# Two of sixteen modulation blocks computed by one-column matmuls in a fused transformer layer

## The chip, the cores and the metric

The kernel runs on one core of a Trainium2 chip. The metric is the device time of one execution in microseconds (us). The core has a matrix engine (TensorE, PE in the profile; its weight loads are listed as PEld), a vector engine (VectorE, DVE), a scalar engine (ScalarE, ACT), GpSimd (POOL) and a queue engine (SyncE, SP) that issues the transfers from memory. Each engine works through its own list of instructions in order; semaphores join them.

## The reference, cut to what matters

One layer of a conditioned decoder trunk with 512 tokens (T) and width 2048 (D). What the change touches is the first statement of it:

```python
cond = jax.nn.silu(c)                         # (1, 2048)
mod = (cond @ ada_w + ada_b)                  # (1, 12288) = 2048 x 12288 weights, f32, 96 MiB
sh1, sc1, g1, sh2, sc2, g2 = jnp.split(mod, 6, axis=-1)
h = rms_norm(x, norm_mix) * (1.0 + sc1) + sh1 # (512, 2048)
proj = h @ w_in                               # 2048 x 4416
# ... attention, state-space mixer, output projection, expert layer, final norm
```

The first 128 of the 2048 columns of h need the first 128 values of sc1 and of sh1, and so on in 16 blocks of 128. Each of those values is a dot product of 2048 elements.

## The kernel before, in words

Everything is kept transposed: a tile has 128 channels on its partitions and the 512 tokens along its rows. The 16 channel blocks of x are called dc = 0 to 15 below.

The input stage is the block under the pool "start". It loads x (16 tiles of 256 KB), squares each tile on ScalarE and adds the squares up on VectorE (xsq). `rstd_rows` then sums them over the partitions with four one-column matmuls (L293), refines a reciprocal square root in a few tiny VectorE operations (L297 to L303), and spreads it over the partitions with four more matmuls (L306). ScalarE copies the outcome to `rb1` (L309). VectorE multiplies each of the 16 x tiles with `rb1` (L331); these are the norm products.

The modulation comes from `ada_vec` (L242 to L251). `cond`, the 2048 values of silu(c), lies on all 128 partitions. A row block of the transposed weight, 128 outputs by 2048 inputs and 1 MiB, is loaded in two halves (tile `at`, 8 buffers of 512 KB). VectorE multiplies each half with `cond` and sums along the row in the same pass (L248). For each dc there are two row blocks, scale and shift, so four passes, and then two tiny operations that join the halves and add the bias (L250, L251) into `mod[dc]`.

For each dc the loop then loads a 512 KB block of the input projection's weight and splits it into a high part (`wh`, a ScalarE copy, L260) and a low part (`wl`, a VectorE subtraction, L261), three buffers each. It forms `A` (L336), applies scale and shift on ScalarE (L337), and splits h into `ah` (ScalarE, L338) and `al` (VectorE, L340). Eight output blocks are accumulated in the eight PSUM banks at once, so each dc gives TensorE 24 matmuls of 128 x 512 (L265 to L267: wh with ah, wh with al, wl with ah). The banks are read when dc 15 is done, and the state-space mixer starts from them.

The order of each engine's list is not written out by hand. A scheduler places the instructions by their data, their priority (the weight split has high priority) and its own estimate of time, and from then on the list is fixed. All loads of this stage go through the one SP queue in the order of its list; a load whose buffer is still in use holds up every load behind it.

Of the kernel before, what the change touches and what calls it, by code (L numbers as in the profile page):

```python
# [9 lines left out]
F32 = mybir.dt.float32  # L10
# [3 lines left out]
AF = mybir.ActivationFunctionType  # L14
ALU = mybir.AluOpType
# [5 lines left out]
D = 2048  # L21
# [17 lines left out]
G0 = 0  # L39
GEND = 333  # L40
EPS = 1e-6
BIG = 1e30

C_ID, C_TRI, C_TRIS, C_IOTA = 0, 128, 256, 384
C_SUB = 512
C_C = 768
# [11 lines left out]
C_ADAB = C_CMASK + 1  # L58
# [19 lines left out]
def layout(x, c, ada_w, ada_b, norm_mix, norm_ffn, w_in, cmp_pe, cmp_w1, cmp_w2, rel_bias,  # L78
           attn_out_norm, conv_w, conv_b, dt_bias, a_log, d_skip, ssm_norm, w_out,
           peer_wq, peer_subkeys, peer_u, peer_v, norm_final):  # L80
    f = np.float32
    a = {}
    a["xT"] = np.ascontiguousarray(x[0].T.reshape(16, 128, T))
    aw = ada_w[0].T.reshape(6, 16, 128, D)
    ab = ada_b[0].reshape(6, 16, 128)
    pairs = [((1, j), (0, j)) for j in range(16)]
    pairs += [((2, 2 * j), (2, 2 * j + 1)) for j in range(8)]
    pairs += [((4, j), (3, j)) for j in range(16)]
    pairs += [((5, 2 * j), (5, 2 * j + 1)) for j in range(8)]
    ada = np.empty((96, 128, D), f)  # L90
    adab = np.zeros((128, 96), f)
    for j, pr in enumerate(pairs):
        for k, (v, dc) in enumerate(pr):
            ada[2 * j + k] = aw[v, dc]
            adab[:, 2 * j + k] = ab[v, dc]
    a["ada"] = ada
    a["c"] = c
    w = w_in[0]
    q0, kv0, g0, z0, xb0, dt0 = 0, 1024, 1792, 1840, 2864, 4400
    B0, C0 = xb0 + 1024, xb0 + 1280  # L100
    dtg = np.zeros((D, 128), f)
    dtg[:, 0:16] = w[:, dt0:dt0 + 16]
    dtg[:, 32:80] = w[:, g0:g0 + 48]
    first = np.stack([w[:, B0:B0 + 128], w[:, B0 + 128:B0 + 256], w[:, C0:C0 + 128], w[:, C0 + 128:C0 + 256],
                      dtg, w[:, xb0:xb0 + 128], w[:, z0:z0 + 128], w[:, xb0 + 128:xb0 + 256]], 1)
    a["w8"] = np.ascontiguousarray(first.reshape(16, 128, 8, 128))
    starts = [z0 + 128]
    for p in range(2, 8):
        starts += [xb0 + 128 * p, z0 + 128 * p]
    starts += [kv0 + 128 * i for i in range(6)]  # L110
    starts += [q0 + 128 * i for i in range(8)]
    a["win"] = np.stack([w[:, s:s + 128].reshape(16, 128, 128).transpose(1, 0, 2) for s in starts])

    def nblocks(m):
        return np.ascontiguousarray(m.reshape(16, 128, -1, 128).transpose(2, 1, 0, 3))
    wo = np.concatenate([w_out[0][1024:], w_out[0][:1024]], 0)
    a["wo"] = nblocks(wo)
    a["wq"] = nblocks(peer_wq[0])
    a["ut"] = np.ascontiguousarray(peer_u[0].reshape(128, 128, 16, 128).transpose(0, 3, 2, 1))
    a["un"] = peer_u[0]  # L120
    a["vn"] = peer_v[0]
    pv = peer_v[0].reshape(128, 128, 8, 256)
    vd = np.zeros((128 + WIN - 1, 128, WIN, 256), f)
    for k in range(128 + WIN - 1):
        c0, c1 = window(k)
        vd[k, :, :c1 - c0] = pv[c0:c1, :, k % 8].transpose(1, 0, 2)
    a["vd"] = vd
    a["cw1"] = np.ascontiguousarray(cmp_w1[0].reshape(2, 16, 128, 256).transpose(0, 2, 1, 3))
    a["cw2"] = np.ascontiguousarray(cmp_w2[0].reshape(2, 2, 128, 64).transpose(0, 2, 1, 3))
    cst = np.zeros((128, C_END), f)  # L130
    r = np.arange(128)
    cst[:, C_ID:C_ID + 128] = np.eye(128)
    cst[:, C_TRI:C_TRI + 128] = r[:, None] <= r[None, :]
    cst[:, C_TRIS:C_TRIS + 128] = r[:, None] > r[None, :]
    cst[:, C_IOTA:C_IOTA + 128] = r[None, :]
    cst[:, C_SUB:C_SUB + 128] = peer_subkeys[0, 0].T
    cst[:, C_SUB + 128:C_SUB + 256] = peer_subkeys[0, 1].T
    cst[:, C_C:C_C + 16] = _cols(c[0])
    cst[:, C_NM:C_NM + 16] = _cols(norm_mix[0])
    cst[:, C_NF:C_NF + 16] = _cols(norm_ffn[0])  # L140
    cst[:, C_NO:C_NO + 16] = _cols(norm_final)
    cst[:, C_AON:C_AON + 8] = _cols(attn_out_norm[0])
    cst[:, C_SSN:C_SSN + 8] = _cols(ssm_norm[0])
    cst[:, C_CW:C_CW + 48] = conv_w[0].reshape(4, 12, 128).transpose(2, 1, 0).reshape(128, 48)
    cst[:, C_CB:C_CB + 12] = _cols(conv_b[0])
    cst[:, C_DSK:C_DSK + 8] = _cols(np.repeat(d_skip[0], 64))
    cst[0:16, C_DTB] = dt_bias[0]
    cst[0:16, C_ALOG] = a_log[0]
    cst[:, C_CMASK] = r >= NCMP
    cst[:, C_ADAB:C_ADAB + 96] = adab  # L150
    cst[:, C_PE:C_PE + 32] = cmp_pe[0].reshape(2, 16, 128).transpose(2, 0, 1).reshape(128, 32)
    a["cst"] = cst
    rb = np.zeros((32, 16 + 640 + 640), f)
    rb[:, :16] = rel_bias
    bk = _buckets()
    for j in range(512):
        rb[bk[511 - j], 16 + j] = 1.0
    rb[:16, 16 + 640 + 512:] = BIG
    a["rb"] = rb
    return a  # L160
# [6 lines left out]
def build(tc, nc, I, out, dbg=None, stop=None):  # L167
    dbg = dbg or {}
    es = ExitStack()
    V, S, PE, G, SP = nc.vector, nc.scalar, nc.tensor, nc.gpsimd, nc.sync  # L170
# [14 lines left out]
    def col(base, i=0, n=1):  # L185
        return cst[:, base + i:base + i + n]
# [7 lines left out]
    mod = [cp.tile([128, 2], F32, name=f"mod{j}") for j in range(48)]  # L194
# [9 lines left out]
    def mm_():  # L204
        return bank("mm", 3)

    def s_():
        return bank("s", 2)

    def t_():  # L210
        return bank("t", 2)

    def o_():
        return bank("o", 1)
# [10 lines left out]
    cond = adp.tile([128, D], F32, name="cond")  # L225
# [64 lines left out]
    def rstd_rows(dst, ssq, n, scale=1.0):  # L290
        pc = t_()
        for tb in range(4):
            PE.matmul(pc[:, tb:tb + 1], ssq[:, 128 * tb:128 * tb + 128], ones[:, 0:1], start=True, stop=True)  # L293
        v = cp.tile([128, 4], F32, name="rv_", tag="rv_", bufs=2)
        r = cp.tile([128, 4], F32, name="rr_", tag="rr_", bufs=2)
        w = cp.tile([128, 4], F32, name="rw_", tag="rw_", bufs=2)
        V.tensor_scalar(v, pc[:, 0:4], scale / n, EPS, op0=ALU.mult, op1=ALU.add)  # L297
        S.activation(r, v, AF.Sqrt)
        V.reciprocal(r, r)  # L299
        V.tensor_tensor(w, r, r, op=ALU.mult)  # L300
        V.tensor_tensor(w, w, v, op=ALU.mult)
        V.tensor_scalar(w, w, -0.5, 1.5, op0=ALU.mult, op1=ALU.add)
        V.tensor_tensor(r, r, w, op=ALU.mult)  # L303
        pr = t_()
        for tb in range(4):
            PE.matmul(pr[:, 128 * tb:128 * tb + 128], r[:, tb:tb + 1].to_broadcast([128, 128]), ident,  # L306
                      start=True, stop=True)
        if dst is not None:
            S.copy(dst, pr)  # L309
        return pr  # L310

    hH, hL = act_tiles()

    with tc.tile_pool(name="start", bufs=1) as sp:
        xs = []
        xsq = sp.tile([128, T], F32, name="xsq")
        for dc in range(16):
            xt = sp.tile([128, T], F32, name=f"x{dc}")
            SP.dma_start(xt, I["xT"][dc])
            xs.append(xt)  # L320
            sq = sp.tile([128, T], F32, name="sq", tag="sq", bufs=2)
            S.activation(sq, xt, AF.Square)
            if dc == 0:
                V.tensor_copy(xsq, sq)
            else:
                V.tensor_tensor(xsq, xsq, sq, op=ALU.add)
        rb1 = sp.tile([128, T], F32, name="rb1")
        rstd_rows(rb1, xsq, D)
        acc6 = [s_(), s_(), t_(), o_(), mm_(), mm_(), mm_(), t_()]
        for dc in range(16):  # L330
            V.tensor_tensor(xs[dc], xs[dc], rb1, op=ALU.mult)  # L331
        for dc in range(16):
            ada_vec(dc, None, sp, 8)
            hi, lo = wsplit(I["w8"][dc].rearrange("p a b -> p (a b)"), 1024)
            A = sp.tile([128, 1], F32, name="A", tag="A", bufs=4)
            V.scalar_tensor_tensor(A, mod[dc][:, 0:1], 1.0, col(C_NM, dc), op0=ALU.add, op1=ALU.mult)  # L336
            S.activation(xs[dc], xs[dc], AF.Identity, scale=A, bias=mod[dc][:, 1:2])  # L337
            S.copy(hH[dc], xs[dc])  # L338
            dump("h1", xs[dc], lambda d: d[dc])
            V.tensor_tensor(hL[dc], xs[dc], hH[dc].bitcast(F32), op=ALU.subtract)  # L340
            for b in range(8):
                mm3(acc6[b], hi[:, 128 * b:128 * b + 128], lo[:, 128 * b:128 * b + 128], hH[dc], hL[dc],
                    dc == 0, dc == 15)
# [14 lines left out]
    with ExitStack() as sx:  # L358
        sp = pool(sx, "ssm")
# [79 lines left out]
        for g in range(2):  # L439
# [7 lines left out]
            for c in range(4):  # L447
# [4 lines left out]
                            op=ALU.mult)  # L452
# [854 lines left out]
```

## Time and profile before

| | us |
|---|---|
| median of 3 runs | 3279.59 |
| lowest and highest | 3276.69, 3281.67 |
| the profiled execution's own time | 3287.48 |
| its span | 3285.7 |
| TensorE busy | 3120.6 (95% of the span) |
| VectorE busy | 2730.4 (83%) |
| VectorE passes L248 in the first 240 us | 69, together 82.3 |

The profile page gives busy time of each engine and the span in 40 slices of 82 us; the input stage lies in the first two, where TensorE shows 4 and 9 tenths. A timeline row reads: start, duration, engine, line, operation, out<-in, shape, and in brackets how long the engine had been idle and what released it. Consecutive matmuls overlap, so what a stream of them costs is the distance of the starts and not the duration.

### The profile page before, as it was taken

How to read it: one execution, taken by the hardware profiler on the slowest of the kernel's cores; microseconds unless marked ns; L12 is line 12 of the kernel's file. 1: busy time of each engine (PE TensorE's matmuls, PEld its weight loads, DVE VectorE, ACT ScalarE, POOL GpSimd, SP SyncE). 2: the span in 40 equal slices, each digit the busy share in tenths (PEclk: the TensorE clock that was granted, in tenths of full speed). 3: DMA queues.
4: the chain of work that ended last, by engine and by line, in shares of the span. 5: the costliest groups of instructions: out<-in, count | busy, mean ns of one | idle time of the engine just before them, and what ended most of it. 6: DMA issues, size and time to landing. Idle time of an engine off the chain costs nothing.

```text
span 3285.7 us, 48161 instructions
## 1 busy us (share of the span) xinstructions
PE 3120.6 (95%) x18025; PEld 2869.4 (87%) x18025; DVE 2730.4 (83%) x4763; ACT 1416.2 (43%) x2429; POOL 570.4 (17%) x324
## 2 busy tenths in 40 slices
PE   4999999999999999999998999999999999999996
PEld 3777767877777899988887999999999999999996
DVE  8988879987877899998956988888888888888856
ACT  3443248882263344359874333333333333333332
POOL 0000000000000022231201333333333333333300
PEclk9999999999999999999999999999999999999998
DMA  8746784227822488799967999999989998999853
GB/s 342 285 142 230 249 294 154 91 84 232 297 94 86 143 318 314 278 358 347 344 237 264 368 337 341 341 339 339 342 330 347 342 336 329 343 346 342 330 199 113
DMA packets 256427, 899.30 MB, mean 274 GB/s; under 512 B 23905, under 2 KB 86113, under 8 KB 213025
## 3 DMA queue, kind: packets, MB, share of 16 engines
q1 hardware_dynamic: 209920, 559.35, 48.7%
q0 software_dynamic: 46080, 335.56, 26.3%
q8 instruction: 141, 2.31, 0.3%
q10 hardware_dynamic: 192, 1.31, 0.1%
q14 instruction: 94, 0.76, 0.1%
HBM read 847.82 MB, written 53.55 MB: 274 GB/s over the span
## 4 chain that ended last, share of the span: by engine, by line
PE 70%; DVE 11%; issue 9%; ACT 5%; DMA 4%; POOL 1%; SPq 0%; DVEq 0%; ACTq 0%; POOLq 0%
PE mm L265 10%; PE mm L267 10%; PE mm L266 10%; PE s L266 5%; PE s L265 5%; PE s L267 5%; PE t L266 4%; PE t L265 4%; PE t L267 4%; DVE at L248 2%; PE o L266 2%; PE o L265 2%; PE o L267 2%; DMA wr<-in_ut_dram 1%; ACT stg L1120 1%
## 5 line engine op out<-in xcount | busy, mean ns | idle before, releaser
L876 ACT CAST wh<-wr 128x1024 fp32r<-128x1024 f32 (+1 forms) x550 | 571.6, 1040 | 976.6 <-PE mm L266 436.7
L877 DVE TENSOR_TENSOR wl<-wr,wh 128x1024 fp32r<-128x1024 f32 (+1 forms) x550 | 663.8, 1209 | 337.4 <-ACT wh L876 336.1
L267 PE MATMUL mm<-dh,wl 128*128 128x352 f32 x2048 | 671.8, 328 | 19.7 <-DVE wl L877 19.5
L265 PE MATMUL mm<-dh,wh 128*128 128x352 f32 x2048 | 670.9, 328 | 7.5 <-ACT wh L876 7.5
L266 PE MATMUL mm<-dl,wh 128*128 128x352 f32 x2048 | 667.1, 326 | 0.0
L1032 POOL DMA_INDIRECT rows<-in_un_dram,eidx x128 | 200.9, 1569 | 1796.0 <-DMA wr<-in_ut_dram 1137.9
L267 PEld LDWEIGHTS mm<-dh,wl 128*128 128x128 f32 x2048 | 389.3, 190 | 26.7 <-DVE wl L877 25.8
L265 PEld LDWEIGHTS mm<-dh,wh 128*128 128x128 f32 x2048 | 387.6, 189 | 8.1 <-ACT wh L876 8.0
L266 PEld LDWEIGHTS mm<-dl,wh 128*128 128x128 f32 x2048 | 388.6, 190 | 0.0
L1058 DVE SCALAR_TENSOR_TENSOR facc<-rows,wgt,facc 128x2048 f32<-128x2048 f32 x158 | 370.7, 2346 | 1.7 <-DMA rows<-in_vn_dram,eidxb 0.4
L265 PE MATMUL mm<-ah,wh 128*128 128x512 f32 x864 | 342.9, 402 | 6.6 <-DVE rr__7054 L299 3.3
L266 PE MATMUL mm<-al,wh 128*128 128x512 f32 x864 | 345.5, 400 | 0.0
L267 PE MATMUL mm<-ah,wl 128*128 128x512 f32 x864 | 344.7, 400 | 0.0
L1032 POOL DMA_INDIRECT rows<-in_vn_dram,eidx x128 | 249.2, 1947 | 510.4 <-DVE facc L1058 480.7
L1042 DVE SCALAR_TENSOR_TENSOR rows<-rows,h2t 128x2048 f32<-128x2048 f32 x128 | 291.3, 2282 | 5.0 <-DMA rows<-in_un_dram,eidx 4.9
L248 DVE SCALAR_TENSOR_TENSOR at<-at,cond 128x1024 f32<-128x1024 f32 x192 | 231.5, 1220 | 47.3 <-DMA at<-in_ada_dram 47.0
L265 PEld LDWEIGHTS mm<-ah,wh 128*128 128x128 f32 x864 | 164.3, 190 | 42.0 <-issue 6.0
L267 PEld LDWEIGHTS mm<-ah,wl 128*128 128x128 f32 x864 | 163.6, 189 | 34.6 <-issue 3.0
L266 PEld LDWEIGHTS mm<-al,wh 128*128 128x128 f32 x864 | 163.8, 190 | 34.0 <-issue 3.0
L260 ACT CAST wh<-wr 128x1024 fp32r<-128x1024 f32 x102 | 106.6, 1046 | 163.7 <-PE mm L266 73.5
L261 DVE TENSOR_TENSOR wl<-wr,wh 128x1024 fp32r<-128x1024 f32 x102 | 124.4, 1220 | 25.4 <-ACT wh L260 24.8
L1032 POOL DMA_INDIRECT rows<-in_vn_dram,eidxb x32 | 61.9, 1934 | 121.2 <-DVE facc L1058 110.2
(2965 smaller groups left out, 6679.1 us busy)
## 6 DMA issues: line engine op xcount, KB each, us to landing
wr<-in_ut_dram SPq DMA_DIRECT2D x256, 512.0 KB
wr<-in_vd_dram SPq DMA_DIRECT2D x250, 512.0 KB
at<-in_ada_dram SPq DMA_DIRECT2D x192, 512.0 KB
wr<-in_win_dram SPq DMA_DIRECT2D x54, 512.0 KB
gscr<-stg SPq DMA_DIRECT2D x11, 2048.0 KB
gt<-gscr SPq DMA_DIRECT2D x32, 704.0 KB
wr<-in_wo_dram SPq DMA_DIRECT2D x32, 512.0 KB
wr<-in_wq_dram SPq DMA_DIRECT2D x32, 512.0 KB
```

The lines of the kernel that those rows point to most:

```text
L248: V.scalar_tensor_tensor(at, at, 1.0, cond[:, sl], op0=ALU.mult, op1=ALU.mult, accum_out=acc[:, hf, k:k + 1])
L260: S.copy(hi[:, :n], raw[:, :n])
L261: V.tensor_tensor(lo[:, :n], raw[:, :n], hi[:, :n].bitcast(F32), op=ALU.subtract)
L265: PE.matmul(acc, wh, ah, start=start, stop=False)
L266: PE.matmul(acc, wh, al, start=False, stop=False)
L267: return PE.matmul(acc, wl, ah, start=False, stop=stop)
L876: S.copy(hi[:, :m], raw[:, :m])
L877: ins = V.tensor_tensor(lo[:, :m], raw[:, :m], hi[:, :m].bitcast(F32), op=ALU.subtract)
L1032: G.indirect_dma_start(out=rows, out_offset=None, in_=I["un"] if side == "u" else I["vn"], in_offset=bass.IndirectOffsetOnAxis(ap=ei[:, sl ...
L1042: seq(V.scalar_tensor_tensor(rows, rows, 1.0, h2b if grp else h2t, op0=ALU.mult, op1=ALU.mult, accum_out=dots[:, c:c + 1]))
L1058: seq(V.scalar_tensor_tensor(f, rows, wgt[:, c:c + 1], f, op0=ALU.mult, op1=ALU.add))
L1120: S.copy(stg[:, :, 4 * t4:4 * t4 + 4].rearrange("p a t -> p t a"), gb.rearrange("p (t a) -> p t a", t=4))
```

## The change

The constant `NPE = 2` names two dc blocks, 0 and 1, whose modulation is computed on TensorE. Their four row blocks are laid out a second time (`adat`), with the inputs on the partitions. For each, 16 matmuls with a 128 x 128 f32 weight and one moving column (`cc`, silu(c) as 16 columns) accumulate in one PSUM column. The other 14 blocks of the stage stay on VectorE, each row block now loaded whole (4 buffers of 1 MiB) and taken in one pass of 2048. The row blocks of dc + 3 are written ahead of the weight split of dc, and the norm products stand inside the loop. The later 32 row pairs of the layer still use `ada_vec`.

```diff
+NPE = 2
+    a["adat"] = np.ascontiguousarray(ada[:2 * NPE].reshape(2 * NPE, 128, 16, 128).transpose(0, 3, 2, 1))
     with tc.tile_pool(name="start", bufs=1) as sp:
+        cc = sp.tile([128, 16], F32, name="cc")
+        S.activation(cc, col(C_C, 0, 16), AF.Tanh, scale=0.5)
+        V.scalar_tensor_tensor(cc, cc, 1.0, col(C_C, 0, 16), op0=ALU.add, op1=ALU.mult)
+        V.tensor_scalar(cc, cc, 0.5, None, op0=ALU.mult)
+        pg = mm_()
+
+        def ada_cols(r):
+            at = sp.tile([128, D], F32, name="at", tag="at", bufs=4)
+            SP.dma_start(at, I["adat"][r].rearrange("p a b -> p (a b)"))
+            for q in range(16):
+                PE.matmul(pg[:, r:r + 1], at[:, 128 * q:128 * q + 128], cc[:, q:q + 1], start=q == 0, stop=q == 15)
+            if r % 2:
+                V.tensor_tensor(mod[r // 2], pg[:, r - 1:r + 1], col(C_ADAB, r - 1, 2), op=ALU.add)
+
+        def ada_row(j):
+            acc = sp.tile([128, 2], F32, name="aacc", tag="aacc", bufs=2)
+            for k in range(2):
+                at = sp.tile([128, D], F32, name="at", tag="at", bufs=4)
+                SP.dma_start(at, I["ada"][2 * j + k])
+                V.scalar_tensor_tensor(at, at, 1.0, cond, op0=ALU.mult, op1=ALU.mult, accum_out=acc[:, k:k + 1])
+            V.tensor_tensor(mod[j], acc, col(C_ADAB, 2 * j, 2), op=ALU.add)
+
+        for r in range(2):
+            ada_cols(r)
         xs = []
...
         rstd_rows(rb1, xsq, D)
+        for r in range(2, 2 * NPE):
+            ada_cols(r)
         acc6 = [s_(), s_(), t_(), o_(), mm_(), mm_(), mm_(), t_()]
+        ada_row(NPE)
         for dc in range(16):
             V.tensor_tensor(xs[dc], xs[dc], rb1, op=ALU.mult)
-        for dc in range(16):
-            ada_vec(dc, None, sp, 8)
+            if dc + NPE + 1 < 16:
+                ada_row(dc + NPE + 1)
             hi, lo = wsplit(I["w8"][dc].rearrange("p a b -> p (a b)"), 1024)
```

The scheduler turns this into new lists. Three places of them are spoken of below. Line numbers of the changed kernel differ: the weight split is L262 and L263 there, `A` is L365, `al` is L369, the one-column matmuls are L327, their bias L329, a whole pass L336, its bias L337, a norm product L360.

The first place is VectorE's list at the program's start, ahead of the square sums. Before it reads:

```order
L232 SCALAR_TENSOR_TENSOR cond_124<-ct_131,cond_124 128x1024
L233 TENSOR_SCALAR cond_124<-cond_124 128x1024 x2
L324 COPY xsq_170<-sq_173 128x512
L326 TENSOR_TENSOR xsq_170<-xsq_170,sq_178 128x512
L326 TENSOR_TENSOR xsq_170<-xsq_170,sq_183 128x512
```

In the changed kernel (mm_174 is the PSUM bank that the one-column matmuls write):

```order
L234 SCALAR_TENSOR_TENSOR cond_124<-ct_131,cond_124 128x1024
L235 TENSOR_SCALAR cond_124<-cond_124 128x1024 x2
L329 TENSOR_TENSOR mod0_67<-mm_174,cst_63 128x2
L365 SCALAR_TENSOR_TENSOR A_383<-mod0_67,cst_63 128x1
L350 COPY xsq_212<-sq_215 128x512
L352 TENSOR_TENSOR xsq_212<-xsq_212,sq_220 128x512
```

The bias addition of block 0, which reads what TensorE sums up from the first two row blocks, now stands ahead of all square sums.

The second place is TensorE's list in the changed kernel, from its start to the first matmul of the projection (at_175 and at_193 are the row blocks of dc 0, at_315 and at_333 those of dc 1; xsq_212 the square sums, rr__300 the reciprocal root):

```order
L327 MATMUL mm_174<-cc_170,at_175 128x1 x16
L327 MATMUL mm_174<-cc_170,at_193 128x1 x16
L295 MATMUL t_294<-ones_65,xsq_212 128x1 x4
L327 MATMUL mm_174<-cc_170,at_315 128x1 x16
L308 MATMUL t_309<-cst_63,rr__300 128x128 x4
L327 MATMUL mm_174<-cc_170,at_333 128x1 x16
L267 MATMUL s_352<-ah0_135,wh_379 128x512
```

Before, the two groups of four followed each other and the projection came right behind them. Now sixteen one-column matmuls stand between the two steps of the norm and sixteen more behind them.

The third place is VectorE's list at the end of the stage. Before, the bias of block 15 stands here, with the low part of block 15's weight (wl_1065) two rows behind it:

```order
L251 TENSOR_TENSOR mod15_82<-aacc_1047,cst_63 128x2
L336 SCALAR_TENSOR_TENSOR A_1068<-mod15_82,cst_63 128x1
L261 TENSOR_TENSOR wl_1065<-wr_1062,wh_1064 128x1024
L261 TENSOR_TENSOR wl_1144<-wr_1141,wh_1143 128x1024
L340 TENSOR_TENSOR al15_166<-x15_246,ah15_150 128x512
```

In the changed kernel (wl_908, wl_944, wl_980 are the low parts of the weights of blocks 12, 13 and 14):

```order
L336 SCALAR_TENSOR_TENSOR at_901,aacc_897<-at_901,cond_124 128x2048
L337 TENSOR_TENSOR mod15_82<-aacc_897,cst_63 128x2
L365 SCALAR_TENSOR_TENSOR A_1019<-mod15_82,cst_63 128x1
L263 TENSOR_TENSOR wl_908<-wr_905,wh_907 128x1024
L263 TENSOR_TENSOR wl_944<-wr_941,wh_943 128x1024
L369 TENSOR_TENSOR al15_166<-x15_288,ah15_150 128x512
L263 TENSOR_TENSOR wl_980<-wr_977,wh_979 128x1024
```

The weight split of block 12 now follows the modulation of block 15; before, each block's split followed its own modulation.

## The prediction

> **What bounds the kernel now.** I read the page first (TensorE busy 95% of the span), then the busy time of the first 160 us in windows, then the timelines of TensorE, VectorE and ScalarE in them.
>
> ```profile
> PE 3120.6 (95%) x18025; PEld 2869.4 (87%) x18025; DVE 2730.4 (83%) x4763; ACT 1416.2 (43%) x2429; POOL 570.4 (17%) x324
> 0.00:20.00 20.00, 0.00 (x0) 0.00 (x0) 11.03 (x17) 10.74 (x16) 0.20 (x4) 1.00 0.94 352
> 20.00:40.00 20.00, 3.94 (x16) 3.56 (x16) 18.84 (x40) 8.61 (x13) 0.00 (x0) 1.00 1.03 409
> 40.00:60.00 20.00, 14.64 (x48) 10.97 (x48) 20.00 (x36) 3.78 (x5) 0.00 (x0) 1.00 0.57 196
> 100.00:120.00 20.00, 18.84 (x82) 14.83 (x81) 19.76 (x37) 6.81 (x9) 0.00 (x0) 1.00 1.00 385
> 120.00:140.00 20.00, 16.50 (x70) 12.63 (x69) 19.72 (x38) 7.15 (x9) 0.00 (x0) 1.00 0.77 289
> 140.00:160.00 20.00, 18.02 (x73) 14.29 (x72) 13.94 (x25) 11.70 (x18) 0.00 (x0) 0.91 0.35 108
> 180.00:200.00 20.00, 20.00 (x101) 16.43 (x100) 19.98 (x33) 11.13 (x15) 0.00 (x0) 1.00 0.71 228
> 200.00:220.00 20.00, 14.84 (x65) 10.01 (x64) 16.25 (x40) 9.23 (x14) 0.00 (x0) 0.74 0.19 60
> ```
>
> The columns of the windows are PE, PEld, DVE, ACT, POOL, clock, transfer share, GB/s. From 20 to 140 us VectorE has no idle time to speak of, TensorE has. The transfers run at about 408 GB/s, save in 40 to 60 us. From 150 us on TensorE is nearly full until a hole of 5 us at 200 to 220. So the stage's end sets when everything behind it starts, and the stage is VectorE's. One block of it, from one `A` to the next:
>
> ```profile
> 134.17 0.16 DVE L336 SCALAR_TENSOR_TENSOR A<-mod,cst 128x1 f32<-128x1 f32 x1
> 134.28 1.22 DVE L261 TENSOR_TENSOR wl<-wr,wh 128x1024 fp32r<-128x1024 f32 x1
> 136.56 0.69 DVE L340 TENSOR_TENSOR al<-x,ah 128x512 fp32r<-128x512 f32 x1
> 137.17 1.22 DVE L248 SCALAR_TENSOR_TENSOR at<-at,cond 128x1024 f32<-128x1024 f32 x1
> 138.31 0.08 DVE L248 DVE_READ_ACCUMULATOR at<-at,cond 128x1 f32 x1
> 138.31 1.22 DVE L248 SCALAR_TENSOR_TENSOR at<-at,cond 128x1024 f32<-128x1024 f32 x1
> 141.11 0.16 DVE L336 SCALAR_TENSOR_TENSOR A<-mod,cst 128x1 f32<-128x1 f32 x1
> ```
>
> A half pass takes 138.31 - 137.17 = 1.14 us of VectorE, `wl` and `al` 1.14 and 0.61, the block 6.94. TensorE needs less and waits:
>
> ```profile
> 117.92 0.39 PE L266 MATMUL t<-al,wh 128*128 128x512 f32 x1
> 120.21 0.39 PE L266 MATMUL t<-al,wh 128*128 128x512 f32 x1
> 128.94 0.73 PE L265 MATMUL s<-ah,wh 128*128 128x512 f32 x2 [1.17 <-ACT ah L338]
> 143.63 0.92 PE L265 MATMUL s<-ah,wh 128*128 128x512 f32 x2 [1.98 <-ACT ah L338]
> 144.35 0.63 PE L265 MATMUL t<-ah,wh 128*128 128x512 f32 x1
> 147.34 0.44 PE L267 MATMUL s<-ah,wl 128*128 128x512 f32 x1
> 147.61 0.39 PE L266 MATMUL t<-al,wh 128*128 128x512 f32 x1
> 150.60 0.39 PE L267 MATMUL t<-ah,wl 128*128 128x512 f32 x1
> ```
>
> The first two rows are ten starts apart: 0.229 us each, 24 x 0.229 = 5.5 us a block. Behind the last `A` (141.1) only block 15 is left, and the stage ends at 151.0. The granted clock stands at 0.91 in 140 to 160; here the matmuls after a 1.98 us gap last 0.63, and 0.39 again 3.9 us later.
>
> **The change, part by part.** I call M the time at which block 1's bias (L329) is through on VectorE, since all passes stand behind it.
>
> (1) The two row blocks on TensorE. A one-column matmul with a 128 x 128 f32 weight is in the trace, two records each:
>
> ```profile
> 26.74 1.86 PE L293 MATMUL t<-ones,xsq 128*128 128x1 f32 x8 [26.74 <-DVE xsq L326]
> 742.92 0.95 PE L293 MATMUL t<-ones,oss 128*128 128x1 f32 x8
> 6.90 2.00 ACT L231 ACTIVATE ct<-cond 128x1024 f32<-128x1024 f32 x2 [4.88 <-DMA cond<-in_c_dram]
> ```
>
> On an idle engine a record costs (1.86 - 0.35)/7 = 0.216 us (0.35 is the length of one), amid dense work (0.95 - 0.25)/7 = 0.10. So 16 matmuls cost 3.2 to 6.9 us. `cond` lands at 6.9; two MiB at 408 GB/s behind it land at 9.5 and 12.0. The 64 records of block 0 then end at 15.9 if all are fast, at 23.3 if all are slow. No row shows so long a run of them. I take slow for 3.9 us, as in the rows at 143.63 to 147.61, and fast after: 18 slow, 46 fast, 18.0.
>
> The Trainium skill (TensorE: Matmul & The Clock Gate, Part 1) puts the warm-up at about 3.4 us of time whatever the number of matmuls; by that the end would be 17.7, and the sum half a microsecond less. No run here shows whether one-column matmuls count as such time. The same page asks for gaps over about 3 us before the clock falls; the row at 143.63 has it slow after 1.98, so the trace disagrees.
>
> (2) What is queued behind. The bias of block 0 stands ahead of `xsq`, so VectorE idles from the end of `cond` until then.
>
> ```profile
> 11.47 0.42 DVE L324 COPY xsq<-sq 128x512 f32<-128x512 f32 x1
> 21.36 1.22 DVE L248 SCALAR_TENSOR_TENSOR at<-at,cond 128x1024 f32<-128x1024 f32 x1
> 28.64 0.16 DVE L297 TENSOR_SCALAR rv__257<-t 128x4 f32<-128x4 f32 x1 [0.81 <-PE t L293]
> 34.50 2.07 PE L306 MATMUL t<-cst,rr__258 128*128 128x128 f32 x8 [5.90 <-DVE rr__258 L303]
> 37.24 7.31 DVE L331 TENSOR_TENSOR x<-x,rb 128x512 f32<-128x512 f32 x12
> ```
>
> Thirteen of the square sums took 21.36 - 11.47 = 9.9 us, the other three at 0.8 make 12.3. With 0.3 for bias and `A`, `xsq` ends at 18.0 + 0.3 + 12.3 = 30.6 (28.5 to 35.9; it was 26.7). The four matmuls L293 take 1.9 more. Then TensorE has row block 2 ahead of the spreading of the root, slow again until 30.6 + 3.9 = 34.5: 10 slow, 22 fast, 36.8. The tiny operations of the root run beside that. Spreading 0.8, row block 3 3.2, bias 0.3: M = 41. All fast it is 37, all slow 53.6. SP has the third and fourth whole-row loads and the first projection weight behind the release of these buffers; they land within 6 us of their issue, ahead of the passes that use them, so I cost that at nothing; if not, it adds to M.
>
> (3) VectorE from M to the last `A`. Left are 14 norm products (7.31/12 = 0.61) 8.5; 28 whole passes; 12 `wl` 13.7; 15 `al` 9.2; 14 pairs of bias and `A` at 0.4, 5.6. A whole pass is bounded by
>
> ```profile
> L1042 DVE SCALAR_TENSOR_TENSOR rows<-rows,h2t 128x2048 f32<-128x2048 f32 x128 | 291.3, 2282 | 5.0 <-DMA rows<-in_un_dram,eidx 4.9
> L248 DVE SCALAR_TENSOR_TENSOR at<-at,cond 128x1024 f32<-128x1024 f32 x69 | 82.3, 1217 | 0.0
> L337 ACT ACTIVATE x<-x,mod,A 128x512 f32<-128x512 f32 x16 | 12.9, 814 | 52.1 <-DVE A L336 51.4 <-DVE x L331 0.8
> ```
>
> The half pass occupies 0.07 less than its mean, so 2.28 - 0.07 = 2.21, against 2 x 1.14: 28 x 2.21 = 62. That also means that whole rows save only 0.07 a pair, 2 us in all. `al` now stands right behind `wl`, while ScalarE needs 0.81 + 0.62 from `A` to `ah`: a wait of 0.5 in some nine blocks, 4.3. Sum 103, a block 7.0, where it was 6.94. The last `A` is at 41 + 103 = 144; it was at 141.1, so taking two of sixteen blocks away buys nothing on this engine, because the wait of (2) and the norm products inside the loop eat it.
>
> (4) The tail. At the last `A`, TensorE still lacks the low part for block 12. Four blocks follow instead of one: 4 x 5.5 = 22 us, where the split of blocks 13 to 15 (1.14 each) is no bound. The stage ends at 144 + 22 = 166 against 151.0: +15. With M = 37 it is +11.
>
> (5) Behind the stage. The state-space chain starts from the same last block in both, and TensorE is full in between, so I carry the 15 us through. Two half passes fewer stand in VectorE's list ahead of the 5 us hole at 200 to 220; they could give back 2.3. No other cover is there.
>
> The sum is made against the profiled execution (3287.48, span 3285.7), which lies 7.9 above the median of the three runs. The same 15 on the median, 3279.59, gives **3295 us**.
>
> **The rivals.** *All slow.* The one-column matmuls never raise the clock, since a moving column is so little work. M = 53.6, the last `A` 156.6, the end 178.6: +27.6, 3302 to 3307 with (5). For it: all eight records at 26.74 are slow. Against it: 1.86 us is shorter than the 3.9 that the full matmuls needed. It decides within the first 14 us: the bias of block 0 at 23.5 and not 18.
>
> *Absorbed.* The matmuls cost 0.10 or less from the start, M = 35 or earlier, and the hole at 200 to 220 takes 5 or more: +9 - 5 = +4, 3280 to 3284. For it: that hole belongs to VectorE's list, and the lists are rearranged up to about 400 us. Against: what starts the chain there is the end of the stage itself.
>
> *The transfers set the end (faster).* This listing of transfers, 0 to 145 us in 40 slices, shows their hole:
>
> ```profile
> GB/s 135 412 399 388 397 409 409 411 408 407 410 408 42 0 209 264 328 414 406 411 410 406 414 407 409 411 406 401 393 346 380 389 400 349 390 359 385 93 64 99
> ```
>
> Slices 13 and 14 (43.5 to 50.75) are nearly empty, since VectorE took twelve norm products in one go and freed no buffer. If the stage followed the transfers, spreading the products would close that hole: 7 us faster, 3272. Place: the SP list at the third whole-row load. It decides there: that load must be issued before the one ahead of it has landed (about 32.6), so row block 2 must be off TensorE by 32; I have it at 36.8. Against it too: VectorE's 20.00 of 20 in just those windows.
>
> **How the numbers follow.** The forecast has 0.5 (its own range 3288 to 3299, from M = 37 with 2.3 given back to M = 45, slow spells half as long again), all slow 0.3, absorbed 0.1, faster 0.06, anything else 0.04. A measurement of this kernel tells 0.2% (6.6 us) from no change. Faster by more: 0.07, the third rival and a little. Within: 0.10, the second. Slower: 0.83. The range for 8 in 10 takes the forecast and most of the slow rival: 3285 to 3308.
>
> **What would show it.** Right: block 0's bias on VectorE at 17 to 19, `xsq` ending near 31, the bias of block 1 near 41, the first 128 x 512 matmul about 14 later (two more norm products, three passes and ScalarE's third block stand ahead of the first weight split), blocks of 7.0 in the middle with waits of TensorE for `wl`, and four blocks on TensorE behind the last `A`. Wrong: the tail shorter than 15 us, which would need a split earlier than the list has it; a whole pass far from 2.21; or a hole at 200 to 220 that shrinks by more than 2.3. If the middle blocks are 7.5 or more, TensorE falls to the slow clock in each of its 1.5 us gaps, which I hold unlikely since the 1.17 us gaps did not do it.

## The result and the profile after

The changed kernel is slower: median 3315.48 us of 4 runs (3313.02 to 3317.09), where the kernel before had 3278.64 of 4 (3276.69 to 3281.67) beside it. The ratio is 1.0110, with a 95% interval of 1.0098 to 1.0123; the difference is 36.8 us. The forecast was 3295, so the direction was right and the size less than half of what came. The two profiled executions lie closer together: 3315.54 with a span of 3313.7, against 3287.48 with 3285.7, which is 28.0 us.

The timelines of the changed kernel's first 70 us come first, TensorE and VectorE:

```profile
9.52 13.79 PE L327 MATMUL mm<-cc,at 128*128 128x1 f32 x64 [9.52 <-DMA at<-in_adat_dram]
36.02 1.87 PE L295 MATMUL t<-ones,xsq 128*128 128x1 f32 x8 [12.72 <-DVE xsq L352]
37.75 6.97 PE L327 MATMUL mm<-cc,at 128*128 128x1 f32 x32
44.58 2.05 PE L308 MATMUL t<-cst,rr__300 128*128 128x128 f32 x8
46.42 6.83 PE L327 MATMUL mm<-cc,at 128*128 128x1 f32 x32
67.00 0.79 PE L267 MATMUL s<-ah,wh 128*128 128x512 f32 x1 [13.75 <-ACT wh L262]
```

```profile
23.34 0.16 DVE L329 TENSOR_TENSOR mod<-mm,cst 128x2 f32<-128x2 f32 x1 [11.79 <-PE mm L327]
24.13 11.83 DVE L352 TENSOR_TENSOR xsq<-xsq,sq 128x512 f32<-128x512 f32 x15
47.28 1.29 DVE L360 TENSOR_TENSOR x<-x,rb 128x512 f32<-128x512 f32 x2 [7.96 <-ACT rb L311]
53.28 0.16 DVE L329 TENSOR_TENSOR mod<-mm,cst 128x2 f32<-128x2 f32 x1 [4.71 <-PE mm L327]
```

All 64 one-column records of block 0 are slow: 13.79 us are 0.215 each. VectorE, whose list has block 0's bias ahead of the square sums, stands still for 11.79 us. The square sums end at 35.96, where they ended at 26.7 before. Then the one-column matmuls of block 1, slow again, stand ahead of the spreading of the root in TensorE's list: VectorE waits 7.96 us for `rb`, and 4.71 for block 1's bias, which is through at 53.4. That is the M of the prediction. The first projection matmul follows at 67.0, 13.7 us behind it.

The middle and the end of the stage, VectorE first, then TensorE:

```profile
128.16 0.69 DVE L369 TENSOR_TENSOR al<-x,ah 128x512 fp32r<-128x512 f32 x1 [0.36 <-ACT ah L367]
128.76 2.28 DVE L336 SCALAR_TENSOR_TENSOR at<-at,cond 128x2048 f32<-128x2048 f32 x1
130.97 2.29 DVE L336 SCALAR_TENSOR_TENSOR at<-at,cond 128x2048 f32<-128x2048 f32 x1
133.50 0.16 DVE L365 SCALAR_TENSOR_TENSOR A<-mod,cst 128x1 f32<-128x1 f32 x1
154.60 0.16 DVE L365 SCALAR_TENSOR_TENSOR A<-mod,cst 128x1 f32<-128x1 f32 x1
```

```profile
155.99 0.74 PE L269 MATMUL s<-ah,wl 128*128 128x512 f32 x2 [1.26 <-DVE wl L263]
176.49 0.40 PE L269 MATMUL t<-ah,wl 128*128 128x512 f32 x1
```

A whole pass costs 130.97 - 128.76 = 2.21 us, and (154.60 - 133.50)/3 = 7.03 us is a block. The last `A` is at 154.6 (141.1 before), and behind it come four blocks on TensorE, 22.3 us. The stage ends at 176.9 where it ended at 151.0: 25.9 us later. That holds most of the loss, and the rest of this text is about where the 25.9 come from and what is lost behind them.

### The profile page after: what moved, and what is told of

Same layout as the page of the kernel before. It is cut to its first block, busy times and chain, and to the rows that moved or that the text cites. A ratio compares the mean times of both kernels' runs of the same rounds, so it can differ in the third digit from the quotient of the medians.

```text
span 3313.7 us, 48277 instructions
## 1 busy us (share of the span) xinstructions
PE 3153.0 (95%) x18153; PEld 2899.8 (88%) x18153; DVE 2719.0 (82%) x4677; ACT 1418.6 (43%) x2430; POOL 571.5 (17%) x324
## 4 chain that ended last, share of the span: by engine, by line
PE 72%; DVE 9%; issue 9%; ACT 5%; DMA 3%; POOL 1%; SPq 0%; DVEq 0%; ACTq 0%; POOLq 0%
PE mm L267 10%; PE mm L269 10%; PE mm L268 10%; PE s L269 5%; PE s L268 5%; PE s L267 5%; PE t L268 4%; PE t L269 4%; PE t L267 4%; PE o L268 2%; PE o L267 2%; PE o L269 2%; DVE at L336 2%; POOL rows L1061 1%; ACT stg L1149 1%
## 5 line engine op out<-in xcount | busy, mean ns | idle before, releaser
L250 DVE SCALAR_TENSOR_TENSOR at<-at,cond 128x1024 f32<-128x1024 f32 x128 | 155.3, 1221 | 43.6 <-DMA at<-in_ada_dram 43.2
L262 ACT CAST wh<-wr 128x1024 fp32r<-128x1024 f32 x102 | 106.8, 1048 | 171.1 <-PE mm L268 103.6
L263 DVE TENSOR_TENSOR wl<-wr,wh 128x1024 fp32r<-128x1024 f32 x102 | 124.2, 1219 | 27.0 <-ACT wh L262 25.0
```

What stands on the lines that cost most here:

```text
L250: V.scalar_tensor_tensor(at, at, 1.0, cond[:, sl], op0=ALU.mult, op1=ALU.mult, accum_out=acc[:, hf, k:k + 1])
L262: S.copy(hi[:, :n], raw[:, :n])
L263: V.tensor_tensor(lo[:, :n], raw[:, :n], hi[:, :n].bitcast(F32), op=ALU.subtract)
```

## The experiments

The kernels were timed in four groups, each with the kernel before beside it on the same chip. "Stage end" is the start of the last projection matmul of the stage plus 0.4, from the one profiled execution; "rest" is the median less the stage end, given as the difference from the same number of the kernel before in its group (whose stage end is taken as 151.0).

| kernel | bias of block 1 on VectorE | last A | stage end | median | ratio to before | rest, against before |
|---|---|---|---|---|---|---|
| before | - | 141.1 | 151.0 | 3278.6 to 3282.9 | 1 | 0 |
| changed | 53.3 | 154.6 | 176.9 | 3315.5 | 1.0110 | +11.0 |
| e9 changed, again | 53.2 | 154.6 | 176.8 | 3312.8 | 1.0103 | +7.3 |
| e2 own row with split | 53.6 | 159.1 | 168.9 | 3299.2 | 1.0051 | -1.6 |
| e3 bias behind the norm | 43.2 | 144.7 | 166.9 | 3301.5 | 1.0058 | +2.7 |
| e4 clock raised first | 50.4 | 151.8 | 174.0 | 3308.5 | 1.0087 | +2.6 |
| e5 e2 and e3 together | 43.2 | 148.9 | 158.8 | 3288.5 | 1.0025 | +0.2 |
| e6 no one-column matmuls | - | 141.8 | 153.1 | 3291.0 | 1.0034 | +8.4 |
| e7 before, whole rows | - | 140.2 | 148.6 | 3279.4 | 0.9997 | +1.3 |
| e8 rows while waiting | 45.7 | 135.3 | 144.6 | 3272.6 | 0.9982 | -1.5 |

### The kernel before, profiled once more

> The kernel before, unchanged, profiled once more. The two profiled executions lie 28.0 us apart in span (3285.7, 3313.7), the timed medians 36.8. Theory A: the first profiled execution of the kernel before was 8 us above its usual runs, somewhere behind the input stage; this one then has a span of 3275 to 3280 and the input stage still ends at 151. Theory B: the profile itself is what differs, and the span is 3284 to 3287 again.

Measured: 3286.99, span 3285.2, beside a median of 3282.91 (3279.14 to 3287.07) in that group. So the two profiled executions of this kernel took 3287.5 and 3287.0, while of the 46 others in the four groups one took 3287.07 and the rest 3272.7 to 3285.0. Profiling does not always lengthen an execution: that of e7 below, 3274.15, is the second shortest of its ten. The stage is the same to 0.1 us up to its last `A` (141.14). One row differs:

```profile
143.66 0.74 PE L265 MATMUL s<-ah,wh 128*128 128x512 f32 x2 [1.97 <-ACT ah L338]
149.07 0.39 PE L267 MATMUL t<-ah,wl 128*128 128x512 f32 x1
```

After the same gap as in the first profile (1.97 here, 1.98 there) the matmuls stay fast here, and the last one starts 1.5 us earlier than the 150.60 of the prediction's row. A stage end read from one execution is good to about that much.

### Each row block in the turn of its own split

```diff
-        ada_row(NPE)
         for dc in range(16):
             V.tensor_tensor(xs[dc], xs[dc], rb1, op=ALU.mult)
-            if dc + NPE + 1 < 16:
-                ada_row(dc + NPE + 1)
+            if dc >= NPE:
+                ada_row(dc)
```

> The changed kernel with one thing undone: the row blocks of a block dc are written in the same turn of the loop as its weight split, not three turns ahead. Theory tail (12.4 us of the loss is that TensorE has four blocks left behind the last A instead of one): the bias of block 1 stays at 53.3, the last A near 154, the stage ends 10 to 11 us behind it near 165 instead of 176.9, time 3301 to 3305. Theory lists (the loss comes from the rearranged lists behind the stage): time stays at 3312 to 3318. Theory front (only the wait ahead of block 1's bias counts, and TensorE catches up): less than 3 us faster.

Measured: 3299.16 (3297.72 to 3302.23), ratio 1.0051, interval 1.0035 to 1.0068. The end of VectorE's and TensorE's stage, last `A`, then TensorE:

```profile
159.06 0.16 DVE L364 SCALAR_TENSOR_TENSOR A<-mod,cst 128x1 f32<-128x1 f32 x1
161.57 0.73 PE L267 MATMUL s<-ah,wh 128*128 128x512 f32 x2 [2.05 <-ACT ah L366]
168.53 0.39 PE L269 MATMUL t<-ah,wl 128*128 128x512 f32 x1
```

The last `A` comes 4.5 us later than in the changed kernel and 5 later than expected: three more splits of 1.14 us stand ahead of it (15 in place of 12), which the expectation left out. And yet the stage ends 8.0 us earlier: the tail is 9.9 us in place of 22.3. The order of rows and splits alone is worth 8 us of the stage, and more of the time: by the ratios, 0.0110 - 0.0051 of 3280, it is 19 us, and the two profiled executions are 13.3 us apart in span (3313.7 and 3300.4). By the profiles 5.3 us of it lie behind the stage, which is taken up below; what goes beyond is seen in the medians alone.

### The bias additions behind the norm

```diff
-            if r % 2:
-                V.tensor_tensor(mod[r // 2], pg[:, r - 1:r + 1], col(C_ADAB, r - 1, 2), op=ALU.add)
+        def ada_bias(j):
+            V.tensor_tensor(mod[j], pg[:, 2 * j:2 * j + 2], col(C_ADAB, 2 * j, 2), op=ALU.add)
...
         for r in range(2, 2 * NPE):
             ada_cols(r)
+        for j in range(NPE):
+            ada_bias(j)
```

> The changed kernel with the two bias additions written behind the norm, so that VectorE's square sums don't wait for the one-column matmuls; everything else as it is. Theory front (the in-order wait ahead of the square sums costs some 10 us): square sums end near 25 instead of 36, block 1's bias at 43 instead of 53.3, stage end near 167, time 3303 to 3307. Theory clock (slow one-column matmuls set it, wherever the bias stands): bias of block 1 still at 50 or later, time within 4 us of 3315.

Measured: 3301.50 (3296.86 to 3303.36), ratio 1.0058, interval 1.0041 to 1.0075. VectorE's timeline:

```profile
14.00 11.84 DVE L353 TENSOR_TENSOR xsq<-xsq,sq 128x512 f32<-128x512 f32 x15 [0.25 <-ACT sq L349]
37.15 1.30 DVE L363 TENSOR_TENSOR x<-x,rb 128x512 f32<-128x512 f32 x2 [7.95 <-ACT rb L311]
43.15 0.23 DVE L330 TENSOR_TENSOR mod<-mm,cst 128x2 f32<-128x2 f32 x2 [4.70 <-PE mm L327]
```

With the two biases out of the way the square sums start at 14.0, and everything after them moves by 9.9 to 10.1 us: block 1's bias, the last `A` (144.7) and the stage end (166.9). The one-column matmuls take exactly as long as before. So step (2) of the prediction, VectorE standing behind the bias of block 0, is worth 10 us here, not the 4 that it was given.

### TensorE's clock raised ahead of the one-column matmuls

```diff
+        wz = sp.tile([128, T], F32, name="wz")
+        V.memset(wz, 0.5)
+        wz_r = sp.tile([128, T], F32R, name="wzr")
+        S.copy(wz_r, wz)
+        pw = mm_()
+        for i in range(NW):
+            PE.matmul(pw, wz_r[:, 0:128], wz_r, start=True, stop=True)
```

> The changed kernel with 23 extra 128 x 512 matmuls on constants ahead of everything on TensorE (their output is read by nobody), which end near 10 us, just when the first row block lands. If the one-column matmuls then keep the fast clock: 0.10 us a record, block 0's bias at 16 to 17, and if rows 2 and 3 are slow again, block 1's bias near 47, time 3307 to 3311. If the clock falls although TensorE has no gap: the first records 0.11, later ones 0.216, block 0's bias at 19 to 22, time 3311 to 3315. Which of the two it is tells whether a run of one-column matmuls counts as work for the clock.

NW is 23, and what these matmuls write is read by nobody. Measured: 3308.52 (3305.6 to 3316.89), ratio 1.0087, interval 1.0069 to 1.0105. TensorE's busy time in windows (then its granted clock, transfer share, GB/s), and the row of the timeline:

```profile
8.00:11.00 3.00, 3.00 (x22) 1.00 1.01 425
11.00:14.00 3.00, 3.00 (x22) 0.75 1.03 387
14.00:17.00 3.00, 3.00 (x16) 0.50 1.04 385
17.00:20.00 3.00, 3.00 (x15) 0.50 1.05 388
```

```profile
9.41 11.00 PE L335 MATMUL mm<-cc,at 128*128 128x1 f32 x64
```

The dense matmuls raise the clock, the one-column matmuls begin fast, 0.11 us from start to start, and about 3 us later, at 12.5, the granted clock falls to 0.50 although TensorE has not been idle for a moment. From there on a record takes as long as in the changed kernel. This is the second of the two cases that were expected. Block 0 is through 2.9 us earlier, and so is all that follows up to the last `A` (151.8).

### The clock held by wider matmuls

```diff
                 PE.matmul(pg[:, r:r + 1], at[:, 128 * q:128 * q + 128], cc[:, q:q + 1], start=q == 0, stop=q == 15)
+                if r < 2 and q % 2:
+                    PE.matmul(pw[:, 0:256], at[:, 128 * q:128 * q + 128], at[:, 0:256], start=True, stop=True)
```

> The changed kernel with 23 matmuls of 512 columns ahead of the one-column ones (as in e4) and, among the one-column matmuls of block 0, one fp32 matmul of 256 columns behind every second of them (16 in all); what these write is read by nobody. In e4 the one-column records ran at 0.095 us for 3 us and then at 0.215. Theory 'one-column matmuls do not hold the clock': with wider ones between them the fast state stays, the 64 one-column records cost 0.10 us each and the 32 wide ones 0.11 to 0.23, so block 0 is through at 19 to 23. Rival 'the clock falls some 3 us after the dense block whatever follows, or it is held low by the input stage': slow from 12.5 on, 1.7 us for each pair with its wide matmul, block 0 through behind 30.

Measured: one execution, 3310.02, span 3306.8. Rows of the timeline, the last of the 16 turns, and a window:

```profile
22.21 0.50 PE L335 MATMUL mm<-cc,at 128*128 128x1 f32 x4
22.57 0.68 PE L337 MATMUL mm<-at 128*128 128x256 f32 x2
23.09 0.50 PE L335 MATMUL mm<-cc,at 128*128 128x1 f32 x4
```

```profile
20.00:23.00 3.00, 3.00 (x21) 1.00 1.08 408
```

Four one-column records cost 22.57 - 22.21 = 0.36 us, 0.09 each (0.11 from start to start, the first of the four close behind its wide neighbour), up to the last of them, and the granted clock is 1.00 throughout. So the clock is not lost with time or by the place in the program: one-column matmuls do not hold it, and wider ones among them do. Block 0 was through at 23.6, a little past the 19 to 23 that were expected, since a wide record took 0.26 and not up to 0.23. As a remedy it is worth nothing: block 0 was through at 23.3 in the changed kernel, so the wide matmuls use up what the fast records save. (The stage ends at 174.1, 2.8 us before the changed kernel's, since here the scheduler put some of the square sums ahead of block 0's bias.)

### Both orders undone together

The edits of e2 and e3 in one kernel.

> Two edits to the changed kernel together: block 1's and block 0's bias add stand behind the norm (as in e3), and each block's rows are written in its own loop turn (as in e2). The one-column matmuls stay, and run at 0.215 us a record. Theory 'order': the loss comes from those two places in VectorE's list, and the two are independent. The bias of block 1 at 43.3 (e3), from it to the last A 105.5 us (e2: 53.6 to 159.06), so the last A at 148.8; 9.7 us from there (e2: 159.06 to 168.8), stage end 158.5, 7.5 us behind the kernel before; some 2 to 3 given back behind the stage as in e2 and e3, so 5 us slower than before, ratio 1.0010 to 1.0025. Rival 'either is enough': the two undo the same delay, and together they are no faster than e2 or e3 alone, ratio 1.005.

Measured: 3288.50 (3282.71 to 3292.42, 10 runs), ratio 1.0025, interval 1.0015 to 1.0035. The last `A` is at 148.87 and the stage end at 158.8, both within 0.3 us of what was worked out, so the two places are independent and their gains add: 9.9 to 10.1 from the bias and 8.0 from the tail make the 18.1 us by which this stage ends earlier than the changed kernel's. The time lies 8.0 us over before, where the stage alone says 7.8; the 2 to 3 us that were to come back behind the stage did not. What is left of the 25.9 us are these 7.8.

### The change without its one-column matmuls

```diff
-NPE = 2
+NPE = 0
```

> The changed kernel with all 16 blocks' modulation as whole rows on VectorE: no one-column matmul, no transposed copy; the products with the norm in the loop and the rows one block ahead stay. Theory 'order': VectorE's start is no longer held by TensorE, and it has two blocks of rows more (8.9 us). xsq ends near 26, the first projection matmul comes before 45 against 67 in the changed kernel, the blocks are 6.7 to 7.0 apart, the last A near 141, a tail of two blocks of 12 us, stage end 151 to 154, time within 4 us of before, ratio 0.999 to 1.002. Rival 'the whole passes and the products in the loop cost by themselves': stage end behind 160, ratio above 1.003.

All 16 blocks are whole rows on VectorE (the loop over block 0's `ada_cols` is taken out too); rows ahead and products inside the loop stay. Measured: 3291.01 (3289.43 to 3297.90, 5 runs), ratio 1.0034, interval 1.0020 to 1.0047. The stage is as expected (first projection matmul at 38.0, last `A` 141.8, end 153.1, which is 2.1 us over before), but the time is not: it is 10.5 us over before. By the medians 8.4 of that are lost behind the stage; the two profiled executions are only 3.5 us apart in span (3289.2 and 3285.7), 1.4 of it behind the stage.

### The kernel before with whole rows and the products in the loop

```diff
             V.tensor_tensor(xs[dc], xs[dc], rb1, op=ALU.mult)
-        for dc in range(16):
-            ada_vec(dc, None, sp, 8)
+            ada_row(dc, sp)
```

> The kernel before with two parts of the change and without its one-column matmuls: each row in one pass of 2048 elements with four buffers, and the products with the norm inside the block loop; rows written in their own turn as before. By the rows of both kernels a whole row is 2.21 us where two halves are 2.29, and one add of 0.2 us a block goes, but the changed kernel's blocks are 7.04 us apart where those of before are 6.94, since the low part of the activation waits 0.36 us for ScalarE there while before a half pass fills that wait. So theory 'the pass is worth nothing here': 0 to 2 us slower, ratio 0.9995 to 1.001. Rival 'the pass gains what its rows say': 16 blocks of 0.37 us, 6 us less by the stage's end, ratio 0.998 to 0.999.

`ada_row` is that of the change, with the pool as its second argument. Measured: 3279.36 (3274.13 to 3284.29, 10 runs), ratio 0.9997, interval 0.9987 to 1.0006. The last `A` is 0.9 us earlier. So these two parts of the change are worth nothing and cost nothing by themselves; here, with rows in their own turn, the rest shows no loss either.

### Work for VectorE wherever it waited

x is loaded ahead of the transposed rows, these come in 512 KB pieces through the three buffers that are free once `cond` is formed, and the rows and biases are written so that VectorE has a pass to do while it waits:

```diff
+        rstd_rows(rb1, xsq, D)
+        ada_half(2, 0)
+        ada_half(2, 1)
...
+        ada_bias(0)
+        ada_half(3, 0)
+        ada_half(3, 1)
         for dc in range(16):
             V.tensor_tensor(xs[dc], xs[dc], rb1, op=ALU.mult)
+            if dc == 1:
+                ada_half(4, 0)
+                ada_half(4, 1)
+                ada_bias(1)
...
             S.copy(hH[dc], xs[dc])
+            if 4 <= dc < 15:
+                with tc.high_priority():
+                    ada_half(dc + 1, 0)
             V.tensor_tensor(hL[dc], xs[dc], hH[dc].bitcast(F32), op=ALU.subtract)
...
+            if 4 <= dc < 15:
+                ada_half(dc + 1, 1)
```

> One-column matmuls for two blocks as in the changed kernel, but VectorE's list has work at each place where it waited: the squares come first (x is loaded ahead of the transposed rows), both bias adds stand behind the whole rows of blocks 2 and 3, the norm's matmuls are issued between the one-column ones, and from block 4 on the first row of the next block stands between A and the low part. Theory 'order': rows 2 and 3 and twelve products are done by the time block 1's bias comes at 45 to 47, blocks are then 6.6 us apart, the last A is at 134 to 137, stage end 145 to 148 against 151.0, and the time 1 to 5 us under before, ratio 0.9985 to 0.9997. Rival 'TensorE's late start sets the end': four blocks wait for TensorE at 47, stage end not before 151, ratio 1.000 or more.

Measured: 3272.60 (3270.36 to 3286.54, 9 runs), ratio 0.9982, interval 0.9969 to 0.9995. It beats both kernels, the one before by 8 us in the medians (6 by the ratio, with an interval of 1.6 to 10) and the changed one by some 40. VectorE's timeline while TensorE works on the one-column matmuls, and two blocks later on:

```profile
27.08 2.28 DVE L352 SCALAR_TENSOR_TENSOR at<-at,cond 128x2048 f32<-128x2048 f32 x1
45.71 0.22 DVE L337 TENSOR_TENSOR mod<-mm,cst 128x2 f32<-128x2 f32 x2
122.20 0.16 DVE L406 SCALAR_TENSOR_TENSOR A<-mod,cst 128x1 f32<-128x1 f32 x1
122.28 2.28 DVE L352 SCALAR_TENSOR_TENSOR at<-at,cond 128x2048 f32<-128x2048 f32 x1
124.49 0.69 DVE L413 TENSOR_TENSOR al<-x,ah 128x512 fp32r<-128x512 f32 x1
128.75 0.16 DVE L406 SCALAR_TENSOR_TENSOR A<-mod,cst 128x1 f32<-128x1 f32 x1
```

The two biases wait for nothing any more, though block 1's is through only at 45.9. A pass stands between `A` and `al`, so the 0.36 us wait is gone and a block takes 6.55 us where it took 7.03. The last `A` is at 135.3, the stage end at 144.6. The rival had a point: in the windows of this run TensorE is busy without a break from 60 us to the end of the stage.

```profile
60.00:100.00 40.00, 39.82 (x164) 32.23 (x165) 36.60 (x45) 15.27 (x19) 0.00 (x0) 0.96 0.93 367
100.00:140.00 40.00, 40.00 (x173) 32.38 (x172) 38.16 (x49) 16.38 (x21) 0.00 (x0) 1.00 0.83 330
```

So what bounds this stage now seems to be when TensorE gets to the projection; that a faster VectorE would bring little more was not tried.

### The changed kernel again

> The changed kernel as it is, beside the kernel before on one chip, to see how much of the 36.8 us between the two medians stays. The two profiled executions lie 28.0 us apart and the profiled ones of before lie 4 to 9 us over its other executions. Theory 'the profiled execution of before is a long one': the medians differ by 33 to 38 us again, the ratio is 1.010 to 1.0115, and the changed kernel's profiled execution lies within 3 us of its median. Rival 'the difference is 28 and the first comparison drew a low median of before': ratio 1.0080 to 1.0095.

Measured: 3312.78 (3308.89 to 3319.57), against 3279.69 (3275.17 to 3283.99) of before: ratio 1.0103, interval 1.0086 to 1.0119, 33.1 us. Its profiled execution, 3311.00, lies among its others. So the difference between the medians is 33 to 37 us, and the 28.0 between the first two profiles are too small by what the profiled execution of before lies over its other executions.

## Why the prediction failed in size

**Step (1), the price of a one-column matmul, is the step that failed.** It took them as slow for 3.9 us and fast after, by the rows of full matmuls at 143.63 to 147.61. Measured are 0.215 us for every record, 13.8 us where 8.5 were forecast. e4 and e10 show why: records of one column start fast when dense work has raised the clock, fall back within about 3 us without any gap, and stay at 0.09 to 0.11 where wider matmuls stand among them. The Trainium skill (TensorE: Matmul & The Clock Gate, Part 1) says that the warm-up is a span of busy time and no number of matmuls, whatever is issued in it. The traces disagree for one column: 13.8 us without a gap did not raise the clock. The rival "all slow" had the mechanism, with M at 53.6 (measured 53.4), and had it decide in the first 14 us; it was given 0.3. Its own sum, 3302 to 3307, had the stage nearly right (27.6 us later, measured 25.9) and still fell 8 us or more short of the median, for the reasons told under step (5) and behind it. The argument against it, that the eight records at 26.74 were too short to tell, was no evidence against it.

**Step (2), what stands behind them, was right in kind.** VectorE waited at the three places named. With slow records block 0's bias came at 23.3 and not 18.0, the square sums ended at 36.0 and not 30.6, and M was 53.4 and not 41. e3 shows that the first wait alone is worth 10.1 us.

**Steps (3) and (4) held.** From M to the last `A` it was 101.2 us (forecast 103), a pass 2.21 (2.21), a block 7.03 (7.0), the wait for `ah` 0.36 in eight blocks (0.5 in nine), the tail 22.3 (22), the first projection matmul 13.7 us behind M (14). e2 shows the cause of the tail: 9.9 us once each split stands with its own row. The clock did not fall in the 1.26 us gaps, as said. So of the 25.9 us, 12.4 are the mis-sized M, and the other 13.5 are near the forecast's 15.

**Step (5), the stage carried through with up to 2.3 given back, failed too, by less than the medians suggest.** The rest of the kernel is 7 to 11 us longer than before in the medians, not 2 shorter. In the two profiled executions, against which the sum was made, the stage ends 25.9 us later and the kernel 28.0: 2.1 us were lost behind the stage. The other 8.8 of the 36.8 us are what the profiled execution of before (3287.48) lies over its median.

The table shows a pattern: in the four kernels that write rows ahead (changed, e3, e4, e6) the rest is 2.6 to 11.0 us longer, in the four that write them in their own turn (e2, e5, e7, e8) it is between 1.6 shorter and 1.3 longer. By itself this proves little, since the changed kernel's two rows differ by 3.7. The profiled executions show it more clearly. From the stage end to the first matmul that reads `oss` (at 742.92 in the kernel before) it is 590.8 to 595.8 us in changed, e3, e4, e6 and e9, and 584.8 to 588.1 in e2, e5, e7 and e8; from there to the end it is 2539 to 2544 in all nine, without such an order. The two profiled executions of before, 591.9 and 591.0, lie with the first set, though its rows stand in their own turn; whether its shorter executions lie with the second is not on record.

Part of the difference can be seen where the state-space mixer ends. ScalarE's copies `KC` stand there behind the store of the mixer's normed outcome, and TensorE waits for them; its rows in the changed kernel, e3, e4, e6, and then in e2 and e5:

```profile
424.94 0.79 PE L267 MATMUL mm<-ah,wh 128*128 128x512 f32 x1 [4.55 <-ACT KC L602]
```

```profile
413.18 0.50 PE L267 MATMUL mm<-ah,wh 128*128 128x512 f32 x1 [3.50 <-ACT KC L605]
```

```profile
420.94 0.50 PE L268 MATMUL mm<-ah,wh 128*128 128x512 f32 x1 [3.51 <-ACT KC L610]
```

```profile
397.02 0.79 PE L267 MATMUL mm<-ah,wh 128*128 128x512 f32 x1 [3.21 <-ACT KC L600]
```

```profile
412.69 0.50 PE L267 MATMUL mm<-ah,wh 128*128 128x512 f32 x1 [0.74 <-ACT KC L601]
```

```profile
402.53 0.50 PE L267 MATMUL mm<-ah,wh 128*128 128x512 f32 x1 [0.78 <-ACT KC L604]
```

The wait was 0.91 before. Ahead of it VectorE forms the reciprocal root of the mixer's norm, and in the changed kernel three modulation passes for later blocks stand among its tiny operations, two of them waiting for their weights:

```profile
403.21 0.15 DVE L299 TENSOR_SCALAR rv__2824<-t 128x4 f32<-128x4 f32 x1
405.11 1.23 DVE L250 SCALAR_TENSOR_TENSOR at<-at,cond 128x1024 f32<-128x1024 f32 x1 [1.62 <-DMA at<-in_ada_dram]
407.57 1.22 DVE L250 SCALAR_TENSOR_TENSOR at<-at,cond 128x1024 f32<-128x1024 f32 x1 [1.13 <-DMA at<-in_ada_dram]
411.46 0.15 DVE L305 TENSOR_TENSOR rr__2825<-rr__2825,rw__2826 128x4 f32<-128x4 f32 x1
```

From the first to the last of that chain it is 8.3 us here, 6.3 in e3, 6.9 in e4 and 8.0 in e6, against 4.5 before, 4.2 in e2 and 4.4 in e5 (384.05 to 388.42), where two passes stand in it. So a new order in the input stage gave a new order 250 us later. The wait is 2.3 to 3.6 us longer than before's, and the clock falls behind it: for 4 to 7 us the matmuls of these four kernels start 0.43 apart and not 0.23, which is another 2 to 3 us (an estimate from these spacings). What else sets the two groups apart stays open.

**The sum was put on the median as it came from the profile.** That the profiled execution of before lies over its other executions was seen (7.9 us) and taken to hold for both kernels. It did not: the changed kernel's lies within 2 us of its median. Why before's is longer was not found; its timed executions leave no trace. So the 36.8 us are the 15 of the forecast, 10.9 more in the stage (12.4 from M, less 1.5 by which steps (3) and (4) came out shorter), 2.1 behind it, and these 8.8, of which the runs do not show where they arise.

Of the rivals, "the transfers set the end" and "absorbed" fell: row block 2 left TensorE at 44.7 where 32 was needed for the third whole row, the hole behind the stage shrank by 1.2 us only (TensorE idle for 5.2 us in 200 to 220 before, 3.95 in 220 to 240 after), and the delay was carried through.

## What to carry to other kernels

Price an instruction from a row in which it stands in the same company: matmuls of one column were 0.10 us amid dense work and 0.215 in a run of their own, through all 14 us of it. When work moves to another engine, ask first what waits for it in a fixed list; kernels with the same one-column matmuls were 37 us slower, 8 us slower or 6 to 8 us faster than the one before, by the order of the work and the transfers around them. Put work that is ready between a request and the instruction that needs it, and compare whole lists behind the edit too, since the scheduler rearranges them.

## What the runs showed of the hardware

TensorE's clock went down under a run of one-column matmuls, without a gap: 0.11 us a record for 3 us, then 0.215 (e4), and 0.09 to 0.11 for 14 us with wide matmuls among them (e10). The granted clock in the profile's rows does not always tell of it: in the changed kernel the same records are as slow while the column shows 1.00, and 0.50 in e4, where the clock had been high and fell:

```profile
15.00:18.00 3.00, 3.00 (x15) 3.00 (x16) 0.00 (x0) 0.00 (x0) 0.00 (x0) 1.00 1.05 387
```

(The changed kernel, 15 to 18 us; the first value is the width, the next TensorE, the third from the end its clock.) The spacing of the starts is the surer reading.

How long a gap lowers the clock is not one number here: after 1.98 us it was low in one profile of the kernel before, and after 1.97 us it stayed high in another. The fall can also come late. After 3.21 us the first matmul was slow already (e6, 0.79 and then 0.63 us a matmul), while after 3.50 us in e3 the first three were fast and those from 414.28 on slow:

```profile
413.52 0.40 PE L268 MATMUL mm<-al,wh 128*128 128x512 f32 x1
414.28 0.63 PE L268 MATMUL mm<-al,wh 128*128 128x512 f32 x1
```

So the first row behind a gap does not tell whether the clock will stay.
